# When the splits of a newly loaded projection weight begin, and in what order they stand

## The chip, the cores and the metric

The kernel runs on one core of one Trainium2 chip. The metric is the device time of one execution in microseconds (us), lower is better. The kernel before takes 2618.83 us in the median of 3 runs (2616.91 to 2621.61).

## The reference

One layer of a bidirectional encoder with two parallel groups of heads runs over two sequences of 2048 tokens with 1024 features and one set of weights, in fp32:

```
h = rms_norm(x, norm_w);  proj = h @ w_in           # 1024 -> 512|128|128|512 and 4 x 512
q_a, k_a, v_a, g_a, q_b, k_b, v_b, g_b = split(proj)
o_a = windowed_gqa_sink(rope(norm(q_a)), rope(norm(k_a)), v_a, sink) * silu(g_a)   # 8 q heads, 2 kv heads, +-128 tokens
o_b = neighbourhood_attn(norm(q_b), norm(k_b), v_b, rpb_b) * silu(g_b)             # 8 heads, 2-D window of 8 x 16
x = x + concat(o_a, o_b) @ w_out
y = x + (p @ w_ple) * sigmoid(x @ w_ple_gate)
```

## The kernel before

**Tiles and phases.** Tokens are cut into tiles of 128, 16 for each sequence. Phase A makes the projections (`proj_a`) and the windowed attention (`unit_a`) of 32 tiles. Phase B does the same for the neighbourhood attention (`proj_b`, `unit_b`), four heads (a half) at a time: 32 tiles for half 0, and 32 for half 1. In TensorE's program a projection matmul is followed by pieces of attention units by a written plan. Phase C makes the output projection, the gate and the product with w_ple in groups of seven products (`prep` prepares operands, `product` multiplies, `result` takes the sums out).

**Split operands.** Every operand of a matmul is split into a rounded part and a remainder, and a product is three matmuls. A weight is made of blocks of 128x512. A block is loaded raw into the remainder's place (`load_w`, L163 to L172); `split_w` (L144) then casts the rounded part on ScalarE (L146, with the norm's scale, or L150, without) and subtracts on VectorE (L147, L151) for the remainder.

**Changes of weights.** Only one set of projection weights fits: the tags wa0 to wa7 and wb0 to wb7 are written anew three times: from group A to half 0 of group B (about 729 us), from half 0 to half 1 (about 1260 us), and to the output weights (about 1788 us). `paired` does this: it runs the first matmuls of two tiles, calls `load_w` for wa, runs the remaining 48 matmuls of both, and calls `load_w` for wb. A later call with the tags wp0 and wp1 brings w_ple (about 1974 us, phase C).

**What sets the order.** `load_w` issues the DMAs and puts a split job per block into the list `jobs`. `filler` (L839) drives the projections and takes one job out at each fourth matmul; `flush(tag)` takes out all jobs of a tag ahead of its first use. TensorE's order is chained as written. For the other engines a scheduler decides by priority and by when it reckons operands to be ready; an instruction passed through `tc.keep_in_program_order` stays where the program has it. `split_w` has a parameter `pin` for that, used here for a few blocks only. Each engine runs its own list strictly in order.

**Names.** sc and scb are scores (groups A and B), L208 takes their row maximum (mx), L219 and L221 the negated maximum nm, L223 the exponentials on ScalarE; pt and ptb are transposed probabilities, pr and p_t their split copies (L559 ScalarE, L560 VectorE), q the split queries (L245), ot an attention output (L582, L583), o_r an operand of the output projection (L796, L797), opd an operand of phase C (L977, L979, L993), r a result of it (L1054, L1064). xr is a split input tile (L287 ScalarE, L288 GpSimd). `stats_b(s)` (L511) computes 1/rms of a sequence for group B in 14 small VectorE operations (L514 and on, rsqrt L125 to L132); ms_d is its way through memory (L499).

Of the kernel before, what the change touches and what calls it, by code (L numbers as in the profile page):

```python
# [11 lines left out]
F32 = mybir.dt.float32  # L12
F32R = mybir.dt.float32r
I32 = mybir.dt.int32
AF = mybir.ActivationFunctionType
ALU = mybir.AluOpType
# [4 lines left out]
NT = SEQ // 128  # L21
KT = DM // 128
# [45 lines left out]
PD = 9  # L68
PB = (26, 30)
TAIL = 9300  # L70
TW = 256
NU = SEQ // TW
AHEAD = 4
# [15 lines left out]
def emit(ctx, tc, io):  # L89
# [53 lines left out]

    def split_w(w, raw, sc, pin=lambda ins: ins):  # L144
        if sc is not None:
            nc.scalar.activation(w[:, 0], raw, AF.Copy, scale=sc)  # L146
            nc.vector.scalar_tensor_tensor(out=w[:, 1], in0=raw, scalar=sc, in1=w[:, 0].bitcast(F32),  # L147
                                           op0=ALU.mult, op1=ALU.subtract)
        else:
            pin(nc.scalar.copy(w[:, 0], raw))  # L150
            pin(nc.vector.tensor_tensor(out=w[:, 1], in0=raw, in1=w[:, 0].bitcast(F32), op=ALU.subtract))  # L151

    jobs = []

    def pump(n=1):
        for _, job in jobs[:n]:
# [3 lines left out]
    def flush(key):  # L160
        pump(max((i + 1 for i, (k, _) in enumerate(jobs) if k == key), default=0))

    def load_w(pool, tag, src, c0, nk, scaled):  # L163

        ws = []
        for j in range(nk):
            w = pool.tile([128, 2, 512], F32R, tag=f"{tag}{j}", name=f"{tag}{j}", bufs=1)
            raw = w[:, 1].bitcast(F32)
            nc.sync.dma_start(raw, src[128 * j:128 * j + 128, c0:c0 + 512])
            jobs.append((tag, partial(split_w, w, raw, nw[:, j:j + 1] if scaled else None)))  # L170
            ws.append(w)
        return ws  # L172

# [41 lines left out]
    def exps(sm, n, fct, gs, sink=None):  # L215
# [19 lines left out]
                                in1=rd.unsqueeze(2).broadcast_to([128, 4, HD]), op=ALU.mult)  # L235
        sm["g2"] = g2.rearrange("p h d -> p (h d)")
        yield

    P = tc.keep_in_program_order

    def split_q(pqt, q1, q2, part):

# [141 lines left out]
    def proj_a(f):  # L384
# [41 lines left out]
        for i, c in enumerate(project(pq, xr, lambda k, b: w_q[k][:, b, :], 215)):  # L426
            if i in HS and early:
                split(f + 1, HS[i], P)
            if i - 4 in HN and f in last:
                square(f + 1, HN[i - 4])  # L430
            if i == PV:
                values()
            if i == PD and late:
                late.pop()()
            yield c
            if i == ka:
                keys_a(kt, t)
# [31 lines left out]
            regroup(s)  # L469
        else:  # L470
            regroup_next()
        if f == NT + 9:
            stats_b(0)
        yield 0, False

    def combine():
# [127 lines left out]
    def proj_b(f):  # L604
        half, st = divmod(f - 2 * NT, 2 * NT)
        s, j = divmod(st, NT)
        b, cb = divmod(j, 4)
        if f < 2 * NT + 8:
            regroup_next()
        if f == 2 * NT + 9:  # L610
            stats_b(1)
        if not ks_b:
            ks_b.extend(big([128, 32, 2, 64], F32R, f"ks_b{i}") for i in range(2))
        w_qk, w_vg = w_b[half]
        xr = xt.pop(f)
        flush("wa")
        pk = ptile([128, 512], "pj", "pqk")
        for i, c in enumerate(project(pk, xr, lambda k, b: w_qk[k][:, b, :], 215)):
            at = i + 24 if f in last else i
            if at in HX:  # L620
                split(f + 1, HX[at])
            yield c
        sq = ap.tile([128, 512], F32, tag="sq", name="sqb", bufs=2)
        nc.scalar.activation(sq, pk, AF.Square)
        ssq = ap.tile([128, 8], F32, tag="ssq", name="ssqb", bufs=3)
        nc.vector.tensor_reduce(out=ssq, in_=sq.rearrange("p (h d) -> p h d", d=HD), op=ALU.add, axis=AX.X)
        vr = ap.tile([128, 8], F32, tag="vr", name="vrb", bufs=2)
        y = ap.tile([128, 8], F32, tag="y", name="yb", bufs=4)
        nc.vector.tensor_scalar(out=vr, in0=ssq, scalar1=1.0 / HD, scalar2=ep_b[:, st:st + 1],
                                op0=ALU.mult, op1=ALU.add)  # L630
        rsqrt(ap, vr, y, 8, "rqb")
        qg = ap.tile([128, 2, 4, HD], F32, tag="qg", name="qg", bufs=6)
        kt = ap.tile([128, 4, HD], F32, tag="kt", name="kb", bufs=2)
        for dst, c in ((kt, 4), (qg[:, 0], 0)):
            nc.vector.tensor_tensor(out=dst, in0=pk[:, 64 * c:64 * c + 256].rearrange("p (h d) -> p h d", d=HD),
                                    in1=y[:, c:c + 4].unsqueeze(2).broadcast_to([128, 4, HD]), op=ALU.mult)
        yield 0, False
        flush("wb")
        pv = ptile([128, 512], "pj", "pvg")
        for i, c in enumerate(project(pv, xr, lambda k, b: w_vg[k][:, b, :], 215)):  # L640
            if i + 24 in HX and f not in last:
                split(f + 1, HX[i + 24])
            yield c
            if i == (KB if f not in last else 10):
                if f < 2 * NT + 2:
                    pending.append((kt, b, cb))
                else:
                    keys_b(kt, b, cb)
        v = ap.tile([128, 4, 2, HD], F32R, tag="sq", name="vb", bufs=2)
        vp = pv[:, 0:256].rearrange("p (h d) -> p h d", d=HD)  # L650
        nc.scalar.activation(v[:, :, 0, :], vp, AF.Copy, scale=rs_b[:, st:st + 1])
        nc.vector.scalar_tensor_tensor(out=v[:, :, 1, :], in0=vp, scalar=rs_b[:, st:st + 1],
                                       in1=v[:, :, 0, :].bitcast(F32), op0=ALU.mult, op1=ALU.subtract)
        for w, (c0, ncol) in COL_WIN.items():
            lo, hi = max(c0, 16 * cb), min(c0 + ncol, 16 * cb + 16)
            if lo < hi:
                nc.sync.dma_start(v_d[half, s, w][8 * b:8 * b + 8, lo - c0:hi - c0].rearrange("r c h a d -> c r (h a d)"),
                                  v[8 * (lo - 16 * cb):8 * (hi - 16 * cb)].bitcast(F32).rearrange("p h a d -> p (h a d)"))
        gs = qg[:, 1].rearrange("p h d -> p (h d)")
        nc.scalar.activation(gs, pv[:, 256:512], AF.Tanh, scale=hr_b[:, st:st + 1])  # L660
        nc.vector.scalar_tensor_tensor(out=gs, in0=gs, scalar=1.0, in1=pv[:, 256:512], op0=ALU.add, op1=ALU.mult)
        held[f] = qg[:, 0], gs
        next(combining, None)
        yield 0, False
# [97 lines left out]
    def fproj(ps, w, m, xs, nk, mm_):  # L762
        for k in range(nk):
            if mm_ is mm:
                flush(f"o{k // 4}")
                flush(("wa", "wb")[m // 4])
            for i, (a, b) in enumerate(((0, 0), (1, 0), (0, 1))):
                mm_(ps, w[m // 4][k][:, a, 128 * (m % 4):128 * (m % 4) + 128], xs(k, b),
                    start=(k == 0 and i == 0), stop=(k == nk - 1 and i == 2))
                yield 108  # L770
# [69 lines left out]
    def filler(f):  # L840

        gen = proj_a(f) if f < 2 * NT else proj_b(f)
        for n, (cost, last_one) in enumerate(gen):
            if last_one:
                next(gen)
            elif n % 4 == 3:
                pump()
            yield cost

# [68 lines left out]
    with tc.tile_pool(name="c", bufs=1) as op:  # L918
# [192 lines left out]
        for m in range(7 * len(groups)):  # L1111
            n, i = divmod(m, 7)
            stage = groups[n][0]
            if i == 0:
                load_raw(n + 1)
                if stage == 1:
                    load_p(n)
            prep(m + LEAD)
            if m == 4:
                flush("0s4")  # L1120
            if n == 2 and i < 4:
                w_p.extend([load_w(op, "wp0", w_ple_c, 0, 2, False)] if i == 0 else
                           [load_w(op, "wp1", w_ple_c, 512, 2, False)] if i == 1 else [])
                flush(f"wp{i - 2}")
            last_q = {1: (0, 0), 4: (1, 1), 5: (1, 0), 6: (0, 1)}.get(i)
            if stage == 1 and last_q:
                ple_of(n, last_q, 0)
            for mp, ps in product(m):
                if i in (0, 2, 3):
                    result(n, {0: (0, 0), 2: (1, 0), 3: (1, 1)}[i], mp, ps, 0)  # L1130
                else:
                    result(n, last_q, mp, ps, 1)
                if mp == 0 and stage == 1 and last_q:
                    ple_of(n, last_q, 1)
            if n == n_o - 1:
# [81 lines left out]
```

## Time and profile before

| what | value |
|---|---|
| median of 3 runs | 2618.83 us |
| lowest, highest | 2616.91, 2621.61 us |
| the profiled execution's own time | 2626.2 us |
| its span | 2624.4 us |
| TensorE busy | 2552.9 us (97%) |
| VectorE busy | 1959.5 us (75%) |
| ScalarE busy | 1416.7 us (54%) |
| GpSimd busy | 788.5 us (30%) |
| granted TensorE clock, mean | 0.99 |

Busy time on TensorE counts pipelined matmuls, and where the clock is lowered a matmul is busy for longer. In the rows below a line starts with start and duration in us, then engine, source line, operation, out<-in, shape and count; square brackets give the idle time ahead and what released it. PE is TensorE, PEld its weight loads, DVE VectorE, ACT ScalarE, POOL GpSimd, SP the engine that issues DMAs.

### The profile page before, as it was taken

The numbers are of one execution on the slowest core, as the hardware profiler recorded it, in microseconds if no ns is written. First come the engines' busy times: TensorE is split into PE (matmuls) and PEld (weight loads), VectorE is DVE, ScalarE is ACT, GpSimd is POOL, SyncE is SP. The second block draws the span as 40 slices with busy tenths as digits, with TensorE's granted clock in tenths as the row PEclk, the third lists the DMA queues.
The fourth block names the chain that finished last, engine by engine and source line by source line (L and its number), as shares of the span: only waits on it lengthen the run. The fifth ranks groups of instructions, "written<-read, shape, count | busy, mean of one in ns | idle before, by whom it ended". The sixth has DMA issues, their size and how long they took to land.

```text
span 2624.4 us, 46991 instructions
## 1 busy us (share of the span) xinstructions
PE 2552.9 (97%) x16080; PEld 2274.5 (87%) x16080; DVE 1959.5 (75%) x5702; ACT 1416.7 (54%) x3327; POOL 788.5 (30%) x996
## 2 busy tenths in 40 slices
PE   7999999999979999999899999999999999999999
PEld 6888888888867888888788888887999999999999
DVE  6888888888877788888888888888655548555554
ACT  5666666666655566666666666666432214222322
POOL 3332333322323333333233332221122323223321
PEclk9999999999999999999999999999999999999999
DMA  5333322111133555555755555457575446232221
GB/s 176 107 105 105 107 83 93 57 57 59 57 91 118 160 174 170 183 175 157 241 160 162 188 176 152 151 158 214 177 245 183 150 158 208 81 108 97 78 79 47
DMA packets 227520, 357.51 MB, mean 136 GB/s; under 512 B 37937, under 2 KB 115377, under 8 KB 222129
## 3 DMA queue, kind: packets, MB, share of 16 engines
q1 hardware_dynamic: 227280, 354.50, 42.8%
q8 instruction: 128, 2.10, 0.3%
q14 instruction: 112, 0.91, 0.1%
HBM read 266.33 MB, written 105.92 MB: 142 GB/s over the span
## 4 chain that ended last, share of the span: by engine, by line
PE 87%; DVE 6%; DMA 4%; ACT 2%; issue 1%; POOL 0%; SPq 0%; ACTq 0%; DVEq 0%; POOLq 0%
PE pqk L193 13%; PE pvg L193 13%; PE acca L1027 12%; PE accc L1027 9%; PE pg L193 6%; PE pq L193 5%; PE pob L193 4%; PE pple L193 3%; PE scb L193 3%; PE ptb L196 3%; PE sc L193 3%; PE po L193 3%; PE pt L196 3%; PE pk L193 3%; PE pout L193 3%
## 5 line engine op out<-in xcount | busy, mean ns | idle before, releaser
L223 ACT ACTIVATE s<-s,nm 128x384 f32<-128x384 f32 (+4 forms) x512 | 306.4, 600 | 344.3 <-DVE nm L219 185.5
L193 PE MATMUL pvg<-wb,xr 128*128 128x512 f32 x1536 | 458.9, 406 | 0.0
L193 PE MATMUL pqk<-wa,xr 128*128 128x512 f32 x1536 | 436.6, 406 | 0.0
L288 POOL TENSOR_TENSOR xr<-stx,xr 128x512 fp32r<-128x512 f32 x192 | 248.0, 1299 | 205.9 <-ACT xr L287 203.1
L193 PEld LDWEIGHTS pqk<-wa,xr 128*128 128x128 f32 x1536 | 266.8, 189 | 37.2
L193 PEld LDWEIGHTS pvg<-wb,xr 128*128 128x128 f32 x1536 | 270.0, 190 | 32.1
L193 PE MATMUL pg<-wb,xr 128*128 128x512 f32 x768 | 233.0, 411 | 4.3 <-DVE q L445 4.3
L193 PE MATMUL pq<-wa,xr 128*128 128x512 f32 x768 | 223.3, 404 | 3.3 <-ACT wa L146 3.3
L234 POOL TENSOR_TENSOR g<-qg,rd 128x256 f32<-128x256 f32 x64 | 39.4, 615 | 494.0 <-DVE rd L232 480.1
L1027 PE MATMUL acca<-opd,s 128*128 128x256 f32 x1344 | 164.3, 283 | 2.5 <-ACT r L1059 2.5
L193 PEld LDWEIGHTS pq<-wa,xr 128*128 128x128 f32 x768 | 141.5, 192 | 28.1 <-ACT wa L146 3.7
L1027 PEld LDWEIGHTS acca<-opd,s 128*128 128x128 f32 x1344 | 162.6, 192 | 2.9 <-ACT r L1059 2.7
L208 DVE CUSTOM_DVE_ANT_0 s<-scb,bias 128x288 f32<-128x288 f32 (+3 forms) x256 | 141.9, 555 | 28.8 <-PE scb L193 24.5
L193 PEld LDWEIGHTS pg<-wb,xr 128*128 128x128 f32 x768 | 138.6, 191 | 25.2 <-issue 4.6
L721 ACT CAST p_t<-ptb 96x384 fp32r<-96x384 f32 (+3 forms) x256 | 130.0, 509 | 50.1 <-PE ptb L196 48.5
L722 DVE TENSOR_TENSOR p_t<-ptb,p_t 96x384 fp32r<-96x384 f32 (+3 forms) x256 | 149.0, 584 | 9.0 <-ACT p_t L721 6.3
L600 ACT ACTIVATE ks_b<-pktb,wk 64x128 fp32r<-64x128 f32 x256 | 125.5, 490 | 44.4 <-DVE ks_b L601 38.6
L193 PEld LDWEIGHTS pob<-p_t,vw 128*128 128x128 f32 (+2 forms) x832 | 132.6, 189 | 19.0 <-ACT wa L146 0.6
L601 DVE SCALAR_TENSOR_TENSOR ks_b<-pktb,wk,ks_b 64x128 fp32r<-64x128 f32 x256 | 115.1, 449 | 40.1 <-ACT ks_b L600 33.6
L993 POOL TENSOR_TENSOR opd<-sum,opd 128x1024 fp32r<-128x1024 f32 x28 | 69.6, 2486 | 238.1 <-ACT opd L979 238.1
L193 PE MATMUL sc<-ks_a,q 128*128 128x384 f32 (+1 forms) x512 | 122.6, 339 | 18.9 <-DVE pr L560 13.0
L560 DVE TENSOR_TENSOR pr<-pt,pr 128x512 fp32r<-128x512 f32 x184 | 123.4, 682 | 22.9 <-ACT pr L559 22.4
(197 smaller groups left out, 5941.7 us busy)
## 6 DMA issues: line engine op xcount, KB each, us to landing
stx<-x_b SPq DMA_DIRECT2D x128, 256.0 KB
vw<-v_d SPq DMA_DIRECT2D x112, 256.0 KB
stx<-x_a SPq DMA_DIRECT2D x64, 256.0 KB
stn<-x_n SPq DMA_DIRECT2D x64, 256.0 KB
v_d<-vb SPq DMA_DIRECT2D x64, 256.0 KB
x1r<-x_d SPq DMA_DIRECT2D x16, 1024.0 KB
y_t<-r SPq DMA_DIRECT2D x64, 256.0 KB
v_d<-vb SPq DMA_DIRECT2D x96, 128.0 KB
```

What stands on the lines that cost most here:

```text
L193: pinned(nc.tensor.matmul(out, lhsT, rhs, start=start, stop=stop))
L196: pinned(nc.tensor.transpose(out, in_, ident))
L208: nc.vector.tensor_tensor_reduce(out=s[:, :n], in0=ps[:, :n], in1=bias, scale=1.0, scalar=-3.0e38, op0=ALU.add, op1=ALU.max, accum_out=sm[ ...
L223: nc.scalar.activation(ss[i][:, :n], ss[i][:, :n], AF.Exp, bias=nm[:, i:i + 1], accum_out=den[:, i:i + 1])
L288: nc.gpsimd.tensor_tensor(out=lo, in0=raw, in1=hi.bitcast(F32), op=ALU.subtract)
L560: nc.vector.tensor_tensor(out=pr[:, 1], in0=pf, in1=pr[:, 0].bitcast(F32), op=ALU.subtract)
L600: nc.scalar.activation(hi, pkt[a:a + 64, i], AF.Copy, scale=wk[a:a + 64, 1:2])
L601: nc.vector.scalar_tensor_tensor(out=lo, in0=pkt[a:a + 64, i], scalar=wk[a:a + 64, 1:2], in1=hi.bitcast(F32), op0=ALU.mult, op1=ALU.subtract)
L721: nc.scalar.copy(p_t[:kc, :nch, 0], pf)
L722: nc.vector.tensor_tensor(out=p_t[:kc, :nch, 1], in0=pf, in1=p_t[:kc, :nch, 0].bitcast(F32), op=ALU.subtract)
L993: each(lambda x, y, z: eng.tensor_tensor(out=x, in0=y, in1=z, op=ALU.subtract), out, a, b)
L1027: pinned(nc.tensor.matmul(ps[:, kk], w[k][:, a, c:c + 128], o[:, b, k], start=i in (0, 1, 4) and kk == 0 and k == 0 and j == 0, stop=k == ...
```

## The change

After `load_w` the jobs are held for a number of projection matmuls (`HOLD`: 20 for wa, 12 for wb, 0 for wp); then one job is taken at every second matmul. The splits with a scale and those of wp are pinned in program order as well. Jobs have a key for each block; at the use of block k, `ready` takes out the jobs up to block k+1. `stats_b(0)` moves from the end of the projections of tile 25 to the eleventh matmul of its q projection, `stats_b(1)` from the start of tile 41 to behind nine matmuls of it. The number of instructions of TensorE, VectorE and ScalarE stays the same.

```diff
+HOLD = {"wa": 20, "wb": 12, "wp": 0}
...
         if sc is not None:
-            nc.scalar.activation(w[:, 0], raw, AF.Copy, scale=sc)
-            nc.vector.scalar_tensor_tensor(out=w[:, 1], in0=raw, scalar=sc, in1=w[:, 0].bitcast(F32),
-                                           op0=ALU.mult, op1=ALU.subtract)
+            pin(nc.scalar.activation(w[:, 0], raw, AF.Copy, scale=sc))
+            pin(nc.vector.scalar_tensor_tensor(out=w[:, 1], in0=raw, scalar=sc, in1=w[:, 0].bitcast(F32),
+                                               op0=ALU.mult, op1=ALU.subtract))
...
+    jobs, hold = [], [0]
+    P = tc.keep_in_program_order
...
+    def ready(tag, k, w):
+        flush(f"{tag}{k + 1}")
+        flush(f"{tag}{k}")
+        return w[k]
...
     def load_w(pool, tag, src, c0, nk, scaled):
         ws = []
+        hold[0] = HOLD[tag[:2]]
         for j in range(nk):
...
-            jobs.append((tag, partial(split_w, w, raw, nw[:, j:j + 1] if scaled else None)))
+            jobs.append((f"{tag}{j}", partial(split_w, w, raw, nw[:, j:j + 1] if scaled else None, P)))
...
             if i == PD and late:
                 late.pop()()
+            if i == PD + 1 and f == NT + 9:
+                stats_b(0)
             yield c
...
-        if f == NT + 9:
-            stats_b(0)
...
-        if f == 2 * NT + 9:
-            stats_b(1)
...
-        flush("wa")
-        for i, c in enumerate(project(pk, xr, lambda k, b: w_qk[k][:, b, :], 215)):
+        for i, c in enumerate(project(pk, xr, lambda k, b: ready("wa", k, w_qk)[:, b, :], 215)):
+            if i == PD and f == 2 * NT + 9:
+                stats_b(1)
...
-        flush("wb")
-        for i, c in enumerate(project(pv, xr, lambda k, b: w_vg[k][:, b, :], 215)):
+        for i, c in enumerate(project(pv, xr, lambda k, b: ready("wb", k, w_vg)[:, b, :], 215)):
...
-                flush(("wa", "wb")[m // 4])
+                flush(("wa", "wb")[m // 4] + str(KT - 1))
...
-            elif n % 4 == 3:
+            elif hold[0] > 0:
+                hold[0] -= 1
+            elif n % 2:
                 pump()
...
-                flush(f"wp{i - 2}")
+                flush(f"wp{i - 2}1")
```

Where instructions move, the lists of the engines show it. The first place is ScalarE at the first change of weights; the numbered wa names are the eight blocks. Before:

```order
L579 COPY ot<-po 64x256 x2
L245 CAST q_10040<-pqt 64x512
L146 ACTIVATE wa_10115<-wa_10115,nw 128x512
L411 ACTIVATE vv<-pk,y 128x2x64
L146 ACTIVATE wa_10117<-wa_10117,nw 128x512
L245 CAST q_10041<-pqt 64x512
L559 CAST pr<-pt 128x512 x2
L146 ACTIVATE wa_10119<-wa_10119,nw 128x512
L559 CAST pr<-pt 128x512
L146 ACTIVATE wa_10121<-wa_10121,nw 128x512
```

And with the change, where source lines are 6 to 9 lower down:

```order
L586 COPY ot<-po 64x256 x2
L252 CAST q_10040<-pqt 64x512
L418 ACTIVATE vv<-pk,y 128x2x64
L566 CAST pr<-pt 128x512 x3
L448 ACTIVATE sq<-pq 128x512
L252 CAST q_10041<-pqt 64x512
L232 ACTIVATE s,den<-s,nm 128x384 x4
L237 ACTIVATE es<-es 128x4
L586 COPY ot<-po 64x256 x2
L147 ACTIVATE wa_10115<-wa_10115,nw 128x512
L468 ACTIVATE gs<-pg,y 128x512
L147 ACTIVATE wa_10117<-wa_10117,nw 128x512
```

The first two splits stood ahead of the cast of the queries q_10041 and of pr; they now stand behind these, and behind the next unit's exponentials and ot.

The second place is VectorE at the second change, around the first row maximum of a unit of group B (L208 before, L217 after; ISA is its operation). Before, the blocks wa_16585 to wa_16591 stand further up, ahead of these rows:

```order
L741 TENSOR_TENSOR otb<-pob,otb 64x512
L132 SCALAR_TENSOR_TENSOR yb<-rqba,yb 128x8
L601 SCALAR_TENSOR_TENSOR ks_b_10352<-pktb,wk,ks_b_10352 64x16x8
L130 SCALAR_TENSOR_TENSOR rqba<-yb 128x8
L147 SCALAR_TENSOR_TENSOR wa_16593<-wa_16593,nw 128x512
L131 TENSOR_TENSOR rqba<-rqba,vrb 128x8
L601 SCALAR_TENSOR_TENSOR ks_b_10352<-pktb,wk,ks_b_10352 64x16x8
L132 SCALAR_TENSOR_TENSOR yb<-rqba,yb 128x8
L652 SCALAR_TENSOR_TENSOR vb<-pvg,rs_b,vb 128x4x64
L635 TENSOR_TENSOR kb<-pqk,yb 128x256
L208 ISA s,mx<-scb,bias 128x512
```

With the change:

```order
L746 TENSOR_TENSOR otb<-pob,otb 64x512
L608 SCALAR_TENSOR_TENSOR ks_b_10352<-pktb,wk,ks_b_10352 64x16x8
L148 SCALAR_TENSOR_TENSOR wa_16585<-wa_16585,nw 128x512
L608 SCALAR_TENSOR_TENSOR ks_b_10352<-pktb,wk,ks_b_10352 64x16x8
L657 SCALAR_TENSOR_TENSOR vb<-pvg,rs_b,vb 128x4x64
L217 ISA s,mx<-scb,bias 128x512
L217 ISA mx 128x1
L217 ISA s,mx<-scb,bias 128x512
L217 ISA mx 128x1
L666 SCALAR_TENSOR_TENSOR qg<-qg,pvg 128x256
L148 SCALAR_TENSOR_TENSOR wa_16587<-wa_16587,nw 128x512
```

Five splits stood ahead of the first maximum; one does now, and the second stands behind two maxima and a gate operation.

The third place is ScalarE in phase C, at the splits of wp (L150 before, L151 after); the casts to opd are the preparation of the next products. Before:

```order
L979 CAST opd<-sum 128x1024 x4
L150 CAST wp_26172<-wp_26172 128x512
L977 CAST opd<-obr 128x256 x4
L150 CAST wb_25269<-wb_25269 128x512
L150 CAST wb_25271<-wb_25271 128x512
L150 CAST wb_25273<-wb_25273 128x512
L150 CAST wb_25275<-wb_25275 128x512
L150 CAST wp_26174<-wp_26174 128x512
L150 CAST wp_26237<-wp_26237 128x512
L150 CAST wp_26239<-wp_26239 128x512
L979 CAST opd<-oar 128x1024
```

With the change:

```order
L151 CAST wb_25275<-wb_25275 128x512
L986 CAST opd<-oar 128x1024
L984 CAST opd<-obr 128x256 x4
L986 CAST opd<-sum 128x1024 x4
L984 CAST opd<-obr 128x256 x4
L986 CAST opd<-oar 128x1024
L984 CAST opd<-obr 128x256 x4
L986 CAST opd<-sum 128x1024 x3
L151 CAST wp_26172<-wp_26172 128x512
L151 CAST wp_26174<-wp_26174 128x512
L986 CAST opd<-sum 128x1024
L151 CAST wp_26237<-wp_26237 128x512
```

The four wp blocks move behind two to three further preparations; the four wb blocks keep their place between two preparations.

More of the change, by code (lines that the diff above doesn't have):

```diff
@@ L151, in split_w @@
             pin(nc.vector.tensor_tensor(out=w[:, 1], in0=raw, in1=w[:, 0].bitcast(F32), op=ALU.subtract))
-    jobs = []
+    jobs, hold = [], [0]
+    P = tc.keep_in_program_order
     def pump(n=1):
@@ L237, in exps @@
         yield
-    P = tc.keep_in_program_order
     def split_q(pqt, q1, q2, part):
```

## The prediction

> **What bounds the kernel now.** I read the page first, then TensorE's waits, then 4 us windows and the instructions around each wait on a place that the diff touches.
>
> ```profile
> PE 2552.9 (97%) x16080; PEld 2274.5 (87%) x16080; DVE 1959.5 (75%) x5702; ACT 1416.7 (54%) x3327; POOL 788.5 (30%) x996
> PE 87%; DVE 6%; DMA 4%; ACT 2%; issue 1%; POOL 0%; SPq 0%; ACTq 0%; DVEq 0%; POOLq 0%
> ...
> PE sc L193 <- DVE pr L560: 13.0, 4, 11.6
> PE scb L193 <- DVE mx L208: 5.7, 3, 3.7
> PE pout L193 <- DVE o_r L797: 3.3, 3, 2.6
> PE accc L1027 <- ACT opd L979: 3.2, 1, 3.2
> ```
>
> TensorE works nearly throughout and its program does not change, so only its idle time, and a lowered clock behind idle time, can be won. The wait rows give total, times and longest in us. Their longest members, 11.6, 3.7, 2.6 and 3.2 us, lie at the three changes of weights and beside the wp splits. A fifth place, stats_b(0), stands below.
>
> **First change of weights (about 730 to 785 us).** This is the ACT row of the timeline, then VectorE and TensorE, then windows (length, PE, PEld, DVE, ACT, POOL busy, clock, DMA share, GB/s):
>
> ```profile
> 745.69 0.72 ACT L146 ACTIVATE wa<-wa,nw 128x512 fp32r<-128x512 f32 x1 [12.12 <-DMA wa<-w_in_c]
> 747.66 1.29 DVE L560 TENSOR_TENSOR pr<-pt,pr 128x512 fp32r<-128x512 f32 x2 [11.77 <-ACT pr L559]
> 748.50 0.98 PE L193 MATMUL sc<-ks_a,q 128*128 128x384 f32 x2 [11.59 <-DVE pr L560]
> ...
> 736.00:740.00 4.00, 0.91 (x4) 0.39 (x3) 0.00 (x0) 0.00 (x0) 0.01 (x1) 1.00 0.91 17
> 748.00:752.00 4.00, 3.50 (x10) 3.24 (x11) 3.85 (x9) 4.00 (x8) 0.00 (x0) 0.53 0.21 76
> 752.00:756.00 4.00, 4.00 (x19) 3.35 (x18) 3.94 (x18) 2.61 (x9) 0.00 (x0) 1.00 0.00 0
> 756.00:760.00 4.00, 4.00 (x23) 3.27 (x22) 3.91 (x14) 3.20 (x10) 0.96 (x1) 1.00 0.01 2
> 736.00:784.00 48.00, 32.37 (x152) 25.92 (x152) 32.03 (x87) 27.81 (x59) 9.94 (x14) 0.89 0.44 110
> ```
>
> ScalarE stands at its second wa split because that block has not landed; the casts of q and pr queue behind it, VectorE's pr behind those, the scores behind pr. The DMA engines are 91% busy then and move only 17 GB/s. Afterwards TensorE runs 10 and 19 matmuls where the next window has 23: of 4 us that is 2.26 + 0.70 = 2.96, less the 0.50 idle already in the 11.59, so 2.5 us of clock. Removable: 11.6 + 2.5 = 14.1 us. With 20 matmuls held, the casts stand ahead of the splits, so ScalarE passes. The load still lands at 745.7 or so, but its first reader on TensorE comes only behind both tiles' last 48 projection matmuls.
>
> What comes back: eight remainder splits now lie between the pr and row-maximum operations of the next unit instead of running beside an idle TensorE.
>
> ```profile
> L147 DVE SCALAR_TENSOR_TENSOR wa<-wa,nw x16: 735/746/1331, 735.2 to 1285.8; 128x512 fp32r<-128x512 f32 x16
> 768.10 0.73 ACT L146 ACTIVATE wb<-wb,nw 128x512 fp32r<-128x512 f32 x1 [4.28 <-DMA wb<-w_in_c]
> ```
>
> Eight at 0.746 are 6.0 us of VectorE. Following the new order by hand, with these durations, the third score of the unit waits some 3.3 us for its pr, and the wb block returns about 1.3 us beyond the small waits it has now. Gain 14.1 - 3.3 - 1.3 = **9.5**. Bounds: VectorE was busy 32.0 of the 48 us, so at most 16 could go, and the stall with its clock is 14.1; I take 13, one split (0.75) and a little short of that. If all 6.0 us of splits and 2 of the wb block reach TensorE: 14.1 - 8 = 6.
>
> **Second change (1260 to 1320 us).**
>
> ```profile
> 1276.29 1.23 DVE L130 SCALAR_TENSOR_TENSOR rqba<-yb 128x8 f32<-128x8 f32 x1
> 1278.10 1.22 DVE L131 TENSOR_TENSOR rqba<-rqba,vrb 128x8 f32<-128x8 f32 x1
> 1280.75 0.68 DVE L208 CUSTOM_DVE_ANT_0 s<-scb,bias 128x512 f32<-128x512 f32 x1
> 1281.59 0.76 PE L193 MATMUL scb<-ks_b,q1b 128*128 128x512 f32 x1 [3.65 <-DVE mx L208]
> 1303.46 0.47 PE L193 MATMUL scb<-ks_b,q1b 128*128 128x512 f32 x1 [1.53 <-DVE vrb L629]
> ...
> 1280.00:1284.00 4.00, 2.41 (x7) 2.06 (x8) 3.98 (x11) 0.47 (x1) 0.00 (x0) 0.60 0.71 191
> 1284.00:1288.00 4.00, 4.00 (x13) 3.11 (x12) 3.47 (x7) 3.51 (x9) 0.74 (x1) 0.55 0.91 336
> 1288.00:1292.00 4.00, 4.00 (x25) 3.36 (x24) 2.09 (x6) 2.17 (x5) 1.27 (x3) 1.00 0.88 267
> ```
>
> Before the first row maximum VectorE has five splits; the new order has one. Against 25 matmuls in 4 us, the 7 and 13 lost 2.41 - 1.12 = 1.29 and 1.92: 3.2 us of clock, with the 3.65 a total of 6.9. The four splits that move (3.0 us) fall between the other maxima and ahead of the negated maximum, and the exponentials wait for that; I give 1.2 us back at the first transpose and 2.0 at a later stall: 6.9 - 3.2 = **3.7**. Bounds: the whole 6.9 less one split, 6; and 6.9 less eight splits (6.0), 1.
>
> **Third change (1788 to 1830 us).**
>
> ```profile
> 1807.33 0.48 PE L193 MATMUL scb<-ks_b,q1b 128*128 128x512 f32 x1 [1.27 <-DVE mx L208]
> 1819.63 0.51 PE L193 MATMUL pout<-o_r,wa 128*128 128x256 f32 x2 [2.62 <-DVE o_r L797]
> ...
> 1792.00:1796.00 4.00, 4.00 (x23) 3.28 (x22) 2.66 (x7) 3.90 (x11) 2.12 (x4) 1.00 0.94 328
> 1796.00:1812.00 16.00, 14.46 (x74) 11.33 (x72) 15.56 (x44) 10.88 (x24) 0.46 (x2) 1.00 0.70 204
> 1820.00:1824.00 4.00, 3.74 (x21) 3.45 (x20) 3.86 (x9) 3.39 (x8) 0.00 (x0) 0.57 0.59 185
> ```
>
> VectorE is full from 1796 to 1812. Starting the splits later wins the 1.27 at the maximum, but leaves 1.34 us free at 1792 unused and puts as much in front of o_r, where 2.62 us and a clock of .57 already follow. Net **0**, from -2 (1.34 more idle and some clock) to +1.5 (1.27 and a little).
>
> **wp in phase C.**
>
> ```profile
> 1979.63 0.62 ACT L150 CAST wp<-wp 128x512 fp32r<-128x512 f32 x1 [7.23 <-DMA wp<-w_ple_c]
> 1985.24 0.69 DVE L1064 TENSOR_TENSOR r<-accc,r 128x512 f32<-128x512 f32 x1
> 1986.08 6.15 PE L1027 MATMUL accc<-opd,wb 128*128 128x256 f32 x37 [3.17 <-ACT opd L979]
> 1988.00:1992.00 4.00, 4.00 (x25) 4.00 (x25) 2.16 (x3) 0.00 (x0) 0.00 (x0) 0.65 0.37 142
> 1992.00:1996.00 4.00, 4.00 (x35) 4.00 (x35) 2.03 (x5) 1.33 (x4) 0.00 (x0) 1.00 0.36 136
> ```
>
> ScalarE waits 7.2 us for wp's load with the preparation of the next products behind it, and VectorE's r, which frees the accumulator, comes late in turn. Pinned, the wp splits stand several preparations later, when the load is long in. The stall is 3.17; 25 matmuls instead of 35 cost 1.14, and the part of the lowered clock ahead of 1988 some 0.2: **4.5**, at most 4.6, at least 2 if two of the four splits (0.68 us each) meet the next accumulator.
>
> **stats_b(0) (611 to 618 us).**
>
> ```profile
> 618.12 0.62 PE L193 MATMUL sc<-ks_a,q 128*128 128x384 f32 x2 [2.46 <-DVE mx L208]
> 610.00:630.00 20.00, 17.51 (x91) 14.52 (x90) 17.32 (x65) 11.34 (x28) 5.89 (x10) 0.91 0.13 41
> ```
>
> Its 14 small operations stand in one lump ahead of the maxima: 2.46 us idle and 17.5 x .09 = 1.6 of clock, 4.1. Put 10 matmuls into the projection they interleave with another chain of small operations, ahead of ot, which has no slack; I keep 1.1 as lost: **3**, from 0 (the lump only moves) to 4.1. stats_b(1) I put at 0: no wait over 1 us lies at it.
>
> The Trainium skill, "TensorE: Matmul & The Clock Gate", Part 1 (The HAM clock gate), has the clock halve after an idle window of about 3.4 us. Taken as a threshold per stall, it would give no clock back for the stalls of 3.17 and 2.46 us, and the sum would be 3.0 us smaller. The rows above differ: .57 follows 2.62 us and .65 follows 3.17, so I keep the trace's loss.
>
> **Sum:** 9.5 + 3.7 + 0 + 4.5 + 3 = 20.7 us. The profiled execution took 2626.2 us (span 2624.4), 7.4 above the median of 2618.83. It would become 2605.5, and the median 2598; rounded to the cautious side, **2599**.
>
> **Rivals.**
> *VectorE takes it back.* All eight splits reach TensorE at the first change and the low ends hold elsewhere: 6 + 1 - 2 + 2 + 0 = 7, some 2612; with the middle values of the last two, 12.5, so 2606. For it: VectorE is 3.85 to 3.94 of 4 us busy behind the first stall, and 1.2 us operations stand where a GpSimd row of 3.09 us runs. Against: between 736 and 748 it is idle.
>
> ```profile
> 1276.21 3.09 POOL L288 TENSOR_TENSOR xr<-stx,xr 128x512 fp32r<-128x512 f32 x2 [7.85 <-ACT xr L287]
> ```
>
> The Trainium skill, "SBUF — State Buffer", "SBUF: two separate sides", says that a VectorE operation with two SBUF inputs and a GpSimd operation that reads SBUF lock one another out for a whole instruction. The split of 1.331 us agrees, and speaks for this rival.
>
> *Everything comes back.* High ends: 13 + 6 + 1.5 + 4.6 + 4.1 = 29, so 2590. Against it: the splits must run somewhere.
>
> *Slower: pinned splits at the head of the queue.* A pinned split that reaches ScalarE ahead of its load blocks every exponential behind it, with no freedom to pass. The place is wb, held for only 12 matmuls, where a 4.28 us wait stands today. If each of the three changes held ScalarE 12.1 us there as wa's does now, with 2.5 us of clock, 3 x 14.6 = 43.8 is lost against 20.7 won: 2642. It decides from about 8.6 us for each change on ((20.7 + 5.2) / 3).
>
> *The waits only move.* The diff does not do what it says: the load lands no earlier, and if the first stall only moves behind it, 11.2 are left; with the low ends of the others 1 - 2 + 2 + 0 = 1. Between the two I take 4: 2615, within 0.2%. Against it: ScalarE's casts stand ahead of the splits in the new order.
>
> **Chances.** 0.2%, or 5.2 us, is about what a measurement of this kernel can tell from no change. Forecast (13 to 26 won) 0.57; VectorE 0.20; everything 0.08; only moved 0.08; slower 0.07. The first three are faster: 0.85, same 0.08, slower 0.07. The range runs from 2589, just past the case in which everything comes back, to 2613, just past VectorE's low end; the likeliest case alone would be 2593 to 2606.
>
> **What would show it.** Right: no TensorE wait over 5 us near 745; no ACT wait for wa there; a clock of 1.00 in all windows from 736 to 760; new waits of 1 to 3 us on mx, pr or ot there; nothing over 1 us near 1986 and 618. The same matmul count. Wrong: an ACT row of wb waiting over 5 us for its DMA with exponentials behind it; a wait on o_r near 1820 over 4 us; a stall near 745 of over 6 us.

## The result, and the profile after

The changed kernel takes 2603.93 us in the median of 4 runs (2600.93 to 2605.94), the kernel before 2619.32 (2616.91 to 2621.61): a ratio of 0.994, with a 95% interval of 0.9923 to 0.9958. That is 15.4 us less; 20 were forecast, and the time lies inside the range. Beside the experiments below, a second set of executions gave 2606.9 against 2626.38, which is 19.5 us less, a ratio of 0.9924 (0.9907 to 0.994). The two intervals overlap.

The page of the changed kernel, and its TensorE waits (total, times, longest):

```profile
PE 2547.1 (98%) x16080; PEld 2269.7 (87%) x16080; DVE 1963.3 (75%) x5702; ACT 1416.3 (54%) x3327; POOL 789.2 (30%) x996
...
PE pout L202 <- DVE o_r L802: 4.9, 4, 3.5
PE sc L202 <- DVE mx L217: 3.1, 5, 1.0
PE sc L202 <- DVE pr L567: 2.6, 4, 1.2
PE ptb L205 <- ACT s L232: 2.4, 3, 1.0
PE pob L202 <- DVE p_t L727: 2.0, 1, 2.0
```

The 11.6, the 3.7 and the 3.2 us are gone, new waits of 1 to 2 us stand in their places, and the wait on o_r has grown from 2.6 to 3.5. TensorE's work is the same count of matmuls.

**Where the time went.** TensorE's program is the same in both, so the n-th matmul of one trace is the n-th of the other, and the time between two numbers can be subtracted stage by stage. Here are the gains (before minus after, us) of the first pair of profiles, and of a second pair from the runs labelled e1 and e3 below. Stages run between matmuls 3242, 3450 (stats_b), 3890, 4420 (first change), 6600, 6960 (second), 9480, 9800 (third), 10640 and 11000 (wp).

| stage | forecast | first pair | second pair |
|---|---|---|---|
| up to 3242, untouched | 0 | 0.1 | -1.9 |
| stats_b(0) | 3 | 3.9 | 2.3 |
| first change | 9.5 | 13.3 | 11.0 |
| second change | 3.7 | 2.6 | 1.2 |
| third change | 0 | -3.1 | -2.5 |
| wp | 4.5 | 5.2 | 4.2 |
| between and behind these (stats_b(1): 0.8 and 0.7) | 0 | 0.6 | 1.0 |
| sum | 20.7 | 22.7 | 15.3 |

ScalarE and TensorE at the first change, and windows there (length, PE, PEld, DVE, ACT, POOL busy, clock, DMA share, GB/s), changed kernel:

```profile
739.49 0.73 ACT L147 ACTIVATE wa<-wa,nw 128x512 fp32r<-128x512 f32 x1
741.57 0.71 ACT L147 ACTIVATE wa<-wa,nw 128x512 fp32r<-128x512 f32 x1
...
747.97 0.61 PE L202 MATMUL sc<-ks_a,q 128*128 128x384 f32 x2 [0.95 <-DVE mx L217]
763.28 0.62 PE L202 MATMUL sc<-ks_a,q 128*128 128x384 f32 x2 [1.17 <-DVE pr L567]
765.01 0.62 PE L202 MATMUL sc<-ks_a,q 128*128 128x384 f32 x2 [0.87 <-DVE mx L217]
...
732.00:736.00 4.00, 4.00 (x21) 3.48 (x20) 3.97 (x15) 1.58 (x3) 0.61 (x1) 1.00 0.76 14
760.00:764.00 4.00, 2.83 (x14) 1.99 (x12) 4.00 (x8) 3.98 (x8) 0.00 (x0) 1.00 0.02 4
```

The slow stretch of the DMA engines, behind a write of small elements that e7 below singles out, is still there (DMA engines 76% busy at 14 GB/s around 734), but ScalarE's splits have no bracket: nobody waits for a block. VectorE is full instead, and TensorE loses about a microsecond at several places, here at the full clock (in the second pair the clock fell to half for 3.4 us behind the last of them).

At the second change TensorE's rows and one window of the changed kernel are:

```profile
1265.84 0.65 PE L205 MATMUL ptb<-ident,s 128*128 128x128 f32 x4 [1.04 <-ACT s L232]
1271.99 1.14 PE L202 MATMUL pob<-p_t,vw 128*128 128x256 f32 x4 [2.03 <-DVE p_t L727]
1283.20 0.50 PE L202 MATMUL scb<-ks_b,q1b 128*128 128x512 f32 x1 [1.02 <-DVE mx L217]
1289.46 0.66 PE L205 MATMUL ptb<-ident,s 128*128 128x128 f32 x4 [0.91 <-ACT s L232]
...
1272.00:1276.00 4.00, 4.00 (x15) 3.43 (x16) 3.39 (x7) 1.68 (x4) 2.04 (x2) 0.57 0.57 183
```

And at the third, TensorE's longest wait and the windows behind it:

```profile
1799.24 0.80 PE L202 MATMUL pout<-o_r,wa 128*128 128x256 f32 x2 [3.51 <-DVE o_r L802]
...
1796.00:1800.00 4.00, 0.76 (x3) 0.77 (x4) 3.62 (x9) 3.84 (x9) 0.40 (x1) 0.72 1.01 357
1800.00:1804.00 4.00, 3.46 (x17) 3.17 (x16) 3.87 (x9) 1.46 (x4) 0.00 (x0) 0.50 0.58 182
1804.00:1808.00 4.00, 4.00 (x21) 4.00 (x21) 2.58 (x5) 2.80 (x6) 0.00 (x0) 0.50 0.66 160
```

There the clock stays at half for 10.2 us (1797.8 to 1808.0) behind a 3.5 us wait; before it was half for 3.4 us, .57 in one window of 4 us. In phase C the window that had 25 matmuls at .65 now has 36 at 1.00, and no wait is left:

```profile
1964.00:1968.00 4.00, 4.00 (x36) 4.00 (x35) 2.61 (x3) 1.05 (x1) 0.00 (x0) 1.00 1.02 401
```

### The profile page after: what moved, and what is told of

The parts are those of the page before. It is cut to its first block, busy times and chain, and to the rows that moved or that the text cites. A ratio compares the mean times of both kernels' runs of the same rounds, so it can differ in the third digit from the quotient of the medians.

```text
span 2601.7 us, 47013 instructions
## 1 busy us (share of the span) xinstructions
PE 2547.1 (98%) x16080; PEld 2269.7 (87%) x16080; DVE 1963.3 (75%) x5702; ACT 1416.3 (54%) x3327; POOL 789.2 (30%) x996
## 4 chain that ended last, share of the span: by engine, by line
PE 87%; DVE 5%; DMA 2%; ACT 2%; issue 2%; POOL 1%; SPq 0%; POOLq 0%; DVEq 0%; ACTq 0%
PE pqk L202 13%; PE pvg L202 12%; PE acca L1034 11%; PE accc L1034 9%; PE pg L202 6%; PE pq L202 5%; PE pob L202 4%; PE pple L202 3%; PE ptb L205 3%; PE scb L202 3%; PE pt L205 3%; PE po L202 3%; PE sc L202 3%; PE pk L202 3%; PE pout L202 3%
## 5 line engine op out<-in xcount | busy, mean ns | idle before, releaser
L217 DVE CUSTOM_DVE_ANT_0 s<-scb,bias 128x288 f32<-128x288 f32 (+3 forms) x256 | 142.0, 555 | 29.1 <-PE scb L202 23.6
L202 PE MATMUL pob<-p_t,vw 128*128 128x256 f32 (+2 forms) x832 | 141.0, 283 | 2.0 <-DVE p_t L727 2.0
L217 DVE CUSTOM_DVE_ANT_0 s<-sc,mask 128x384 f32<-128x384 f32 (+1 forms) x256 | 135.8, 532 | 0.8
```

The source lines that it names most:

```text
L202: pinned(nc.tensor.matmul(out, lhsT, rhs, start=start, stop=stop))
L217: nc.vector.tensor_tensor_reduce(out=s[:, :n], in0=ps[:, :n], in1=bias, scale=1.0, scalar=-3.0e38, op0=ALU.add, op1=ALU.max, accum_out=sm[ ...
```

## The experiments

The times of before beside these runs are 2625.44 (e1, e5, e6, e7), 2626.38 (e3, e4, e8, e9) and 2625.38 (e2, e10, e11, e12) in the median.

**e1: the kernel before once more.** No edit.

> The kernel before, unchanged, for a second profile. Why: the two profiled executions differ by 22.7 us of span (2624.4 and 2601.7), the medians by only 15.4, and the profiled execution of before was 6.9 us above its median of 2619.3. Theory A (the length of the first stall varies from one execution to the next, since a transfer decides it): the profile here has TensorE's wait at the first change of weights well under 11.6 us, about 5, and all other waits as before, and its span is near 2617. Theory B (the stall is fixed, and the extra time lies elsewhere, spread out): the wait is 11.6 again within 0.5. As timed, the ratio to the kernel before is 1.000 with an interval that shows what three rounds can tell.

Ratio 0.9997 (0.9988 to 1.0006), so three rounds tell about 0.1%. The profile's span is 2620.9, 3.5 us less than the first one's. The waits are the same to 0.3 us; TensorE's rows at the first and the second change, then 2 us windows behind stats_b(0):

```profile
745.86 0.98 PE L193 MATMUL sc<-ks_a,q 128*128 128x384 f32 x2 [11.28 <-DVE pr L560]
1278.39 0.76 PE L193 MATMUL scb<-ks_b,q1b 128*128 128x512 f32 x1 [3.65 <-DVE mx L208]
...
618.00:620.00 2.00, 2.00 (x11) 1.61 (x10) 1.97 (x14) 0.65 (x3) 0.00 (x0) 1.00 0.43 125
620.00:622.00 2.00, 2.00 (x11) 1.66 (x10) 1.80 (x9) 2.00 (x9) 0.00 (x0) 1.00 0.00 0
```

The same two windows of the first profile of before:

```profile
618.00:620.00 2.00, 1.88 (x6) 1.60 (x7) 2.00 (x15) 0.00 (x0) 0.00 (x0) 0.66 0.37 131
620.00:622.00 2.00, 2.00 (x7) 1.52 (x6) 1.87 (x8) 1.99 (x7) 0.00 (x0) 0.50 0.04 8
```

Theory B holds for the waits: they are fixed. What differs between two executions of one kernel is the clock behind them: the same 2.4 us of idle time was followed by a halved clock once and by a full one once. Stage by stage the second execution was shorter by 1.6 us at stats_b(0), 0.8 at the first change, 1.5 at the second and 1.7 at wp, and longer by 0.8 at the third. Of the 1.7 in the stage of wp, 1.4 lie at its start, ahead of the wp splits and behind another wait; the half clock behind the wp stall itself is in both executions.

**e3: the changed kernel once more.** No edit.

> The changed kernel unchanged, beside the kernel before on one chip, with a second profile. Matched matmul by matmul, the first pair of profiles gave 4.4 us at stats_b(0), 12.5 to 13 at the first change, 2.7 at the second, -2.9 at the third and 4.9 at wp. If these are the change and not one lucky profile: the same five numbers within 1 us and a ratio of 0.993 to 0.995, the medians 14 to 20 us apart.

Its ratio stands above, and its stages are the second pair of the table. Four of the five numbers are lower than the first pair's by 1.0 to 2.3 us, the third change by 0.6 less of a loss: signs and sizes hold, "within 1 us" did not.

**e5: pins without a hold.**

```diff
-HOLD = {"wa": 20, "wb": 12, "wp": 0}
+HOLD = {"wa": 0, "wb": 0, "wp": 0}
```

> The changed kernel with all holds at 0: splits pinned in program order, one at every second matmul right behind the load, stats_b moved. On ScalarE the second wa split stands again ahead of the casts of q and pr. If the hold is what takes the first stall away: TensorE's wait near 745 us is back at its length in before, and only the gains at stats_b(0) (4.4 us) and wp (4.9 us) stay: 2619.3 - 9.3, some 2610. If the pinning alone does it: no wait over 2 us there, and a time within 2 us of the changed kernel's 2603.9. If pinned splits at the head of the queue are dangerous, it is slower than 2619.

Median 2623.6, ratio 0.9987 (0.9977 to 0.9996). ScalarE waits for the second block, and TensorE has two stalls in place of one:

```profile
742.17 0.72 ACT L147 ACTIVATE wa<-wa,nw 128x512 fp32r<-128x512 f32 x1 [7.61 <-DMA wa<-w_in_c]
744.28 0.69 PE L205 MATMUL pgt<-ident,g 128*128 128x128 f32 x2 [4.28 <-DVE mx L217]
755.90 0.66 PE L205 MATMUL pt<-ident,s 128*128 128x128 f32 x4 [4.35 <-DVE pr L567]
```

Against e1 the stages are +2.3 (stats_b), +1.3 (first), -5.1 (second), -4.0 (third) and +3.5 (wp). The hold is needed. The expectation of some 2610, 9.3 us under before, was missed: the wait did not come back at its old length, and pinned splits without a hold cost 9 us at the two later changes.

**e6: holds without the pins.**

```diff
-            jobs.append((f"{tag}{j}", partial(split_w, w, raw, nw[:, j:j + 1] if scaled else None, P)))
+            jobs.append((f"{tag}{j}", partial(split_w, w, raw, nw[:, j:j + 1] if scaled else None,
+                                              P if tag[:2] == "wp" else lambda ins: ins)))
```

> The changed kernel with the holds of 20 and 12, but the splits of wa and wb not pinned (those of wp are). The scheduler places the splits of the first change again ahead of the casts, nearly where they stood in before. If the order on ScalarE is the cause and the hold works only through it: the stall near 745 us is back, time some 2610, as without the hold. If it is enough to hand the splits out later: within 2 us of 2603.9.

Median 2615.69, ratio 0.9963 (0.9948 to 0.9978). ScalarE and TensorE at the first change:

```profile
740.99 0.72 ACT L147 ACTIVATE wa<-wa,nw 128x512 fp32r<-128x512 f32 x1 [11.48 <-DMA wa<-w_in_c]
743.05 0.98 PE L203 MATMUL sc<-ks_a,q 128*128 128x384 f32 x2 [10.20 <-DVE pr L568]
```

The scheduler put the later-written splits back where they were. The first change gains 0.7 us, the second 1.1, the third 0; stats_b(0) and wp stay at 2.3 and 3.7. The 0.7 is not the stall's either: behind a wait of 1.5 us near 820 us, which both kernels have, this execution kept the full clock and e1 did not, and that alone is 1.1. So neither half of the change takes the stall at the first change away; hold and pin together do.

**e7: the slow write behind the wa loads, in the kernel before.**

```diff
+            if tag == "wa" and src is w_in_c and c0 == 0:
+                tc.keep_in_program_order(ld)        # ld: the load of a block
...
-        nc.sync.dma_start(ms_d[...], ms_a[:, c])
+        tc.keep_in_program_order(nc.sync.dma_start(ms_d[...], ms_a[:, c]))
```

> The kernel before; only the write of ms_a to memory (2048 elements of 4 bytes, ahead of the second wa load on SP's queue) and the wa loads of the first change are pinned, so that this write is issued behind all eight loads. If that write is what keeps the second block from landing (DMA engines 91% busy at 17 GB/s): the wait at the first change falls from 11.6 us to under 3 with the splits where they were; gain 8 to 12 us in the profile, less what the write then costs the wb loads, 0 to 4. If the loads are late for another reason (the old weights' readers, the time of issue): the wait stays over 9 us, no gain.

Median 2623.94, ratio 0.9995 (0.9985 to 1.0004): no gain, against the expectation. ScalarE, TensorE and the windows say where it went:

```profile
736.61 0.72 ACT L146 ACTIVATE wa<-wa,nw 128x512 fp32r<-128x512 f32 x1 [2.51 <-DMA wa<-w_in_c]
766.07 3.45 ACT L146 ACTIVATE wb<-wb,nw 128x512 fp32r<-128x512 f32 x5 [13.61 <-DMA wb<-w_in_c]
770.17 2.27 PE L198 MATMUL pt<-ident,s 128*128 128x128 f32 x4 [6.60 <-ACT s L225]
...
752.00:756.00 4.00, 4.00 (x14) 3.47 (x13) 2.47 (x7) 0.45 (x2) 0.00 (x0) 0.57 1.29 20
```

The wa wait fell to 2.5 us, as the first theory said, and ScalarE waited 13.6 us for the wb loads behind the write instead, TensorE 6.6 us, after a new wait of 3.2 us for ot near 749 us: the cause is shown, and the stall moves with the write.

**e12: the same edit in the changed kernel.**

> The changed kernel with the write of ms_a issued behind all wa loads and the first four wb loads instead of behind the first wa load. In the kernel before, the same write moved the 11.6 us wait from wa to wb and gained nothing. If pinned splits at the head of ScalarE's list are as sensitive to a late block: ScalarE waits for a wb block by 5 us or more, TensorE loses 4 to 12 us, the kernel is at 2611 to 2619. If wb's splits come late enough: within 3 us of 2606.9, and no wait for a block over 2 us.

Median 2605.15, ratio to before 0.9921 (0.9906 to 0.9936), no different from e3. The only ScalarE wait for a new block (total, times, longest) is:

```profile
ACT wb L147 <- DMA wb<-w_in_c: 1.6, 1, 1.6
```

With the splits far enough behind, the kernel hardly feels where the write stands (the first change is 0.9 us longer than in e3). The danger for which the slower rival spoke did not come even under the later write.

**e9: the slow write cut into one for each tile, in the kernel before.**

```diff
-        nc.sync.dma_start(ms_d[s * SEQ:(s + 1) * SEQ].rearrange("(t p) -> p t", p=128), ms_a[:, c])
...
+        nc.sync.dma_start(ms_d[128 * f:128 * f + 128].rearrange("(t p) -> p t", p=128), ms_a[:, f:f + 1])
```

> The kernel before; the write of ms_a to memory is done tile by tile (16 writes of 128 elements instead of one of 2048), so that only 128 elements stand ahead of the second wa load. The splits, their order on ScalarE and VectorE and all loads stay as before. If that write is the cause of the late block: ScalarE's wait for wa falls from 12 us to under 3, TensorE's 11.6 to under 3, nothing comes back at wb, and the kernel gains 9 to 13 us of 2625, without any hold or pin. If the new weights' loads are slow by themselves: no gain.

Slower: 2638.94, ratio 1.0045 (1.003 to 1.006). The first 600 us, which hold no change of weights, lose 15.5 us, some 9 of them in the one stall at 46 us (11.43 us, where e1 has 2.16), nearly all of it by 190 us. SP's issues and ScalarE ahead of the first change, TensorE at the start, and a window:

```profile
726.98 0.33 SPq L468 DMA_DIRECT2D ms_d<-ms_a  x1
728.42 2.37 SPq L270 DMA_DIRECT2D stn<-x_n  x2
738.44 0.63 ACT L301 ACTIVATE stn<-stn 128x512 f32<-128x512 f32 x1 [4.68 <-DMA stn<-x_n]
46.13 2.47 PE L193 MATMUL pg<-wb,xr 128*128 128x512 f32 x5 [11.43 <-DVE q L445]
...
728.00:732.00 4.00, 4.00 (x20) 3.29 (x19) 3.97 (x15) 1.07 (x4) 2.28 (x3) 1.00 0.94 12
```

Two loads of 256 KB, issued 1.4 us behind a write of only 128 elements, run at 12 GB/s with the DMA engines 94% busy, and ScalarE waits. So a small write is not cheap, the stall at the first change comes back as others (4.8 and 3.9 us), and the run does not isolate what it was made for; that the write is the cause rests on e7.

**e4: the third change as before.**

```diff
+        out_w = src is w_out_c
+        hold[0] = 0 if out_w else HOLD[tag[:2]]
+        every[0] = 4 if out_w else 2       # one job at each fourth matmul; no pin if out_w
```

> The changed kernel, but for the output weights (third change) everything as before: no hold, every fourth matmul, not pinned. If the third change is what loses 2.9 us: the waits there are those of before (1.28 at the row maximum, 2.62 at o_r), the other four places as in the changed kernel, and the time is 2 to 3 us below that of the changed kernel. If the loss is only the phase of the clock: no difference beyond 1 us.

Median 2604.27, ratio to before 0.9918 (0.9903 to 0.9932), 2.6 us under e3, which is not clear of the two intervals. Its waits are those of before, 1.27 and 2.62 us, but for the next one on o_r (0.92 us against 0.26). Against e3 the stage of the third change is 1.2 us shorter; the rest of the 3.0 us of span lies at places with the same order. The 1.2 us are not idle time (5.6 us in the stage, 5.5 in e3) but clock, half for 6.8 us in place of 10.2; and e12, which has e3's order and its 3.5 us wait at the third change, is 1.1 us shorter there with 6.8 us of half clock as well. So that undoing the third change is worth 1.2 us is not shown. By its ratio e4 is the lowest of all variants, within the noise.

**e10: the first change alone** (second and third handed out as before).

> The changed kernel with holds and pins for the first change of weights only; the second and third handed out as before (every fourth matmul, not pinned), wp pinned, stats_b moved. The third undone alone gave 2604.3 beside 2606.9. If the hold is worth 1.1 to 2.7 us at the second change, as the matched traces say: 2605.5 to 2607. If it is worth nothing there, its stalls only moved: 2604.3. If the second change is better off as before: under 2603.

Median 2606.04, ratio 0.9931 (0.9915 to 0.9948), 1.8 us over e4, which the intervals do not tell apart. TensorE has its old wait at the second change:

```profile
1265.60 0.77 PE L205 MATMUL scb<-ks_b,q1b 128*128 128x512 f32 x1 [3.62 <-DVE mx L220]
```

Against e3 the second change is 2.0 us longer and the third 1.6 shorter. The new order (hold, pin and pace together) is worth some 2 us at the second change, 1.0 of it idle time; what it costs at the third, 1.2 us by e4 and 1.6 by this run, is not told apart from the chance of the clock there, by which e12 is 1.1 us shorter with e3's order.

**e8 and e11: other holds for wa**, 32 and 10 instead of 20.

> The changed kernel with a hold of 32 in place of 20 for wa. The splits of the second change then stand behind all four row maxima and the negated maximum, and at the first change behind three casts of pr. If the splits among maxima and exponentials are what gives gain back at the second change (1.0 at ptb, 2.0 at p_t): the 2.7 us there grow to 4 to 6. If VectorE is full in any case: the waits only move on, to the first use of the new weights (pqk) and the unit after it, and the second change gains 0 to 2.7. Whole kernel within 4 us of the changed one.

> The changed kernel with a hold of 10 in place of 20 for wa. At the first change the first three splits stand behind the exponentials, but ahead of the copy to ot and of all pr of that unit. If what counts is that the blocks have landed when ScalarE comes to them: they come some 4 us too early, ScalarE waits 2 to 6 us for its second block, TensorE 1 to 5 behind it, and the kernel is 2 to 6 us slower than with 20. If it is enough that the casts of q and of the first pr stand ahead: within 2 us of 2606.9.

With 32: 2615.58, ratio 0.996 (0.9945 to 0.9975); with 10: 2611.82, 0.9949 (0.9935 to 0.9964); with 20: 2606.9. TensorE with 32 at the second change:

```profile
1283.89 0.73 PE L202 MATMUL pqk<-wa,xr 128*128 128x512 f32 x2 [1.05 <-DVE wa L148]
1295.39 0.66 PE L205 MATMUL ptb<-ident,s 128*128 128x128 f32 x4 [1.69 <-ACT s L232]
1298.64 1.23 PE L202 MATMUL pvg<-wb,xr 128*128 128x512 f32 x2 [2.59 <-DVE wb L148]
```

The splits now come too late for their own users, pqk and pvg, and push those of wb: 3.0 us lost at the first change and 5.0 at the second, against 20. With 10, ScalarE waited 2.0 us for the second block, and at the second change the row maximum waits as in before (3.95 us), since the splits are back ahead of it: 1.3 and 2.4 us lost. 20 lies between two losses. With 32 both expectations failed: the kernel is 8.7 us over that with 20, and the second change loses 3.8 us against e1. With 10 the loss, 4.9 us by the medians, lies in the forecast range of 2 to 6.

**e2: stats_b and wp alone**, on the kernel before.

```diff
+            if i == PD + 1 and f == NT + 9:
+                stats_b(0)
...
+                                      tc.keep_in_program_order if tag[:2] == "wp" else lambda ins: ins)))
```

> The kernel before with two parts of the change alone: stats_b moved into the projections, and the splits of wp pinned in program order. No hold, no other pin. If the five places add up: 2.7 to 4.4 us at stats_b(0) and 4.6 at wp, together 7 to 9 us under the kernel before, and the first three changes of weights as in it (11.3, 3.65 and 2.62 us of wait). If the gains hang together with the holds: less than 5 us.

Median 2617.52, ratio 0.9967 (0.9954 to 0.9979), 7.9 us. The stages give 2.3 and 3.4, and stats_b(1) 0.7; the three changes of weights stay as they were (10.62, 3.64 and 2.62 us of wait). These two parts act by themselves.

## Why the prediction was right, and where not

**First change: mechanism right, size low.** ScalarE passes, the casts come first, and the write that holds the load back is shown by e7. The stall and its clock went: the matmuls around it (3890 to 3996) gain 13.0 and 12.8 us, where the sum has 14.1. The give-back of 4.6 us was too large, it is 0.7 and 2.8: in place of 3.3 us at one score there are waits of 1.17 us and less, and wb gave back nothing. Forecast 9.5, measured 13.3 (just past the bound of 13) and 11.0. Of both, 1.0 is luck: at 823 us both kernels have the same wait of 1.48 us, behind which the clock was half for 3.4 us in before and e1 and full in the two profiles of the changed kernel; but e7, with the old order, keeps it full there, and e4, with the new, does not. "VectorE takes it back", with 6 us, is out here: it is full, but of its 6.0 us of splits only 0.7 and 2.8 came back on TensorE.

**Second change: mechanism right, give-back short.** The 1.2 us at the first transpose and 2.0 at a later stall were seen as 1.04 and 2.03. Not in the sum were the clock that the second of them costs (.57 in the window from 1272) and the next unit's 1.02 and 0.91, where the kernel before had one wait of 1.53. Measured are 2.6 and 1.2 in place of 3.7, and 2.0 by e10.

**Third change: the failed step.** The forecast was 0, bounded at -2; it is -3.1 and -2.5. The bound took 1.34 us more of idle time "and some clock", which leaves 0.7 for the clock. By the rows of VectorE, from the first maximum to the operand o_r that TensorE waits for, seven splits stand now and four before. VectorE in the changed kernel, from the first maximum to that o_r, with the splits:

```profile
1784.23 0.68 DVE L217 CUSTOM_DVE_ANT_0 s<-scb,bias 128x512 f32<-128x512 f32 x1
...
1785.78 1.29 DVE L152 TENSOR_TENSOR wa<-wa 128x512 fp32r<-128x512 f32 x2
...
1787.59 0.69 DVE L152 TENSOR_TENSOR wa<-wa 128x512 fp32r<-128x512 f32 x1
...
1789.72 1.83 DVE L152 TENSOR_TENSOR wa<-wa 128x512 fp32r<-128x512 f32 x2
...
1791.92 0.68 DVE L152 TENSOR_TENSOR wa<-wa 128x512 fp32r<-128x512 f32 x1
...
1794.06 0.68 DVE L152 TENSOR_TENSOR wa<-wa 128x512 fp32r<-128x512 f32 x1
...
1798.76 0.76 DVE L802 TENSOR_TENSOR o_r<-ob,o_r 128x256 fp32r<-128x256 f32 x2
```

The same two operations before:

```profile
1806.49 0.68 DVE L208 CUSTOM_DVE_ANT_0 s<-scb,bias 128x512 f32<-128x512 f32 x1
...
1819.15 0.76 DVE L797 TENSOR_TENSOR o_r<-ob,o_r 128x256 fp32r<-128x256 f32 x2
```

That way takes 14.5 us (1784.23 to 1798.76), against 12.7 before, where splits begin at 1808.12, 1809.95, 1811.47 and 1814.35. The wait grew by 0.9 us and TensorE's idle time in the stage by 0.5 and 0.8, less than the bound had; the clock took the rest and is the term that was too small. It was half for 10.2 us in both profiles of the changed kernel, for 3.4 us in the first profile of before (1820.1 to 1823.5) and for 6.8 in e1 (1813.7 to 1820.5), behind the same wait of 2.62. Part of the loss is therefore chance. Undoing the order (e4, e10) took 1.2 and 1.6 us off, but the stage stays 1.2 and 0.9 us longer than in e1, 0.9 and 0.6 of it idle time; why is open.

**wp and stats_b(0)** came out at 5.2 and 4.2 (forecast 4.5), and 3.9 and 2.3 (forecast 3), and stand alone in e2. At the wp stall alone the two pairs give 4.9 and 4.6; the low end of "at least 2" does not follow from its own terms, since two splits of 0.68 off 4.5 leave 3.1. stats_b(1), put at 0, won 0.7 to 0.8 in both pairs.

**The median.** The sum was made against a profile of 2626.2 us and taken from a median of 2618.83. The first pair of profiles gave 22.7 and the second 15.3; the first medians gave 15.4 and those beside e3 19.5. In the later sets the kernel before took 2625.4 to 2626.4 us in the median, so the profile of 2626.2 is an ordinary execution, while the four executions of the first set (2616.91 to 2621.61) lie below all later ones (2621.9 and up); why is open. The distance of 7.4 us between profile and median, which the prediction carried over, is thus not a property of the kernel. That the sum of 20.7 comes near the 22.7 and the 19.5 is in part luck, since its terms miss in both directions (3.8 us too little at the first change, 3.1 too much at the third, by the first pair). The clock losses in that one profile (1.6 at stats_b, 3.2 at the second change, 1.3 at wp) were read as part of the kernel. In the traces half clock comes in stretches of 3.4 us, or of two, three or four of them in a row, and by estimate one such stretch costs half its length, 1.7 us (1.6 and 1.5 measured, before against e1, where one is missing). Behind the same waits before and e1 differ by one stretch at three places: stats_b(0) has one (618.6 to 622.0) and none, the second change two (1280.8 to 1287.6) and one, the third one and two; at wp both have one (1987.4 to 1990.8, and 1981.0 to 1984.4 in e1). So the clock term of a single stall under 4 us can be off by 1.7 us either way; what it is in the mean of many executions, two cannot tell. The prediction set the rule of 3.4 us aside on the ground that .57 followed 2.62 us. The Trainium skill, "TensorE: Matmul & The Clock Gate", Part 1 (What's actually happening), also says that the window runs freely, so that the count of slow matmuls varies from run to run. The two executions agree: 2.4 us of idle time cost the clock once, and once not.

**The other rivals.** "Everything comes back", that is, no loss anywhere, is out at the second and third changes. "Slower by pinned splits at the head of the queue" is out in the changed kernel (ScalarE's wa splits of the first change show no wait), but e5 shows its start: without the hold the two later changes lose 9.1 us, more than the 7.9 won at the first change, at both places of stats_b and at wp. "The waits only move" is what e7 did, not the change.

## What to carry to other kernels

Where an engine's queue stands behind a load that comes late, moving the transfer may only move the wait to the next load; moving the waiting instruction behind what others need ends it, and here it took both the later hand-out and the pinned order, for the scheduler put the unpinned splits back. The distance has two ends: before the data are there, and before the first user needs the result. Price idle time from one profile, but take a lowered clock behind a stall of a few microseconds as a chance, and look at two executions before it goes into a sum.

## What was not expected of the hardware

Behind the issue of a write of 2048 elements of 4 bytes the DMA engines were 91% busy at 17 GB/s (before), and behind one of 128 elements 94% busy at 12 GB/s (e9). It is not the small elements themselves that take the time: in the trace of before 2080 packets of under 512 bytes moved between 730 and 733 us; from 733 to 743 only 60 packets moved, none under 2 KB, with the engines 57% busy, which by estimate is 1.5 us of engine time for each (0.567 x 16 engines x 10 us / 60), and from 744 to 748 there were 985 at 372 GB/s. Thirty-two small writes in place of two were dearer in e9, though nearly all of that lies in the first 190 us. Why a short write holds the packets behind it for microseconds is not in these traces and stays open.

The wp splits on VectorE, now beside GpSimd's work, take up to 2.9 us, where all four took 0.68 to 0.69 before. The group of these instructions (min, median, max in ns), and VectorE and GpSimd there, changed kernel:

```profile
L152 DVE TENSOR_TENSOR wp<-wp x4: 683/1828/2896, 2029.5 to 2038.6; 128x512 fp32r<-128x512 f32 x4
...
2029.54 3.58 DVE L152 TENSOR_TENSOR wp<-wp 128x512 fp32r<-128x512 f32 x2
...
2029.02 2.40 POOL L1000 TENSOR_TENSOR opd<-sum,opd 128x1024 fp32r<-128x1024 f32 x1 [6.21 <-ACT opd L986]
```

This cost TensorE next to nothing there: its one wait from 2020 to 2045 is 0.31 us. It agrees with what the Trainium skill, "SBUF — State Buffer", "SBUF: two separate sides", says of a VectorE operation with two inputs in SBUF beside a GpSimd operation: one waits out the other.
